# Gate and up projections of four feed-forward blocks by Strassen's seven products, down projection in three chunks

## The chip, the core and the metric

The kernel runs on one core of a Trainium2 chip. The metric is the device time of one execution in microseconds, the median of several. The core's engines run side by side, each in the order of its own list: TensorE (PE, with its weight loads, PEld), VectorE (DVE), ScalarE (ACT), GpSimd (POOL) and SyncE (SP), which issues the transfers. Tiles live in SBUF; TensorE writes into PSUM banks of 128 x 512 numbers.

## What is computed

A two-layer encoder on 512 tokens of width 1024. Each layer is feed-forward (ffn1), attention mixer, attention over a memory, feed-forward (ffn2). The change touches the four feed-forwards only:

```python
def swiglu(x, wg, wu, wd):
    return (jax.nn.silu(x @ wg) * (x @ wu)) @ wd
...
        h = h + 0.5 * swiglu(rmsnorm(h, g), wg, wu, wd)     # ffn1 and ffn2 of each layer, D_FF = 2816
```

## The kernel before

Activations lie transposed: eight tiles `x` of 128 features x 512 tokens. All products are float32 taken apart into two parts that TensorE multiplies fast: `xh` is the rounded tile (ACT), `xl` the rest (DVE), and weights likewise `wh` and `wl`. A product is three matmuls, wh·xh, wh·xl, wl·xh.

A weight tile of 128 x 1024 comes in `wload`: SP issues the transfer into `wf` (three buffers), ACT writes `wh` (L150), DVE writes `wl = wf - wh` (L152); `wh` and `wl` have two buffers each, so that a tile's parts can be made only when the matmuls of the tile two before it are done.

`ffn` runs over 22 blocks f of 128 hidden features. For each, 24 matmuls of 512 columns (8 feature tiles x 3) make the gate and 24 the up projection (L304), each from one weight tile into one bank. The first block's order follows the arrival of the `x` tiles. After the first 24 matmuls of block 1, `stats` transposes on TensorE (L244) the sums of squares `acc`, which ACT and DVE (or POOL) have added up over the eight `x` tiles; DVE reduces them (L246), POOL takes the root, TensorE spreads it over the partitions (L314), and DVE holds it as `R`. `gated` then makes the hidden block: gs = gate·R, tanh, w, us = up·R, h, and the parts `hh`, `hl`. Then `ffn` makes eight output blocks d of 66 matmuls each (L328), with the down weights in pieces of 8, 8 and 6 tiles of 128 x 128, adds the result to `x[d]` (L330), and `made` splits the new `x[d]` and adds its squares for the next norm.

TensorE's order is that of the code. The other engines' lists are set by a scheduler, which puts weight loading and splitting ahead (`high_priority`). Every engine works its list strictly in order. At the start `load_x` interleaves the eight `x` transfers with the first four half tiles of weights. Lines named L... are those of this kernel.

## Time and profile before

| | us |
|---|---|
| median of 3 runs | 2192.61 (2191.3 to 2194.66) |
| the profiled execution | 2188.73 |
| its span, first to last instruction | 2186.9 |

The profile is one execution. Busy times of TensorE are modelled: a matmul's row ends when its result is out, while the next one starts earlier, so the pace is read from starts. "The chain that ended last" follows the span back from its end to whatever released each step.

### The profile page before, as it was taken

What the parts mean: (1) busy time and instruction counts of PE and PEld (TensorE: products, weight loads), DVE (VectorE), ACT (ScalarE), POOL (GpSimd) and SP (SyncE); (2) the same over time, 40 slices, a digit from 0 to 9 for tenths busy, and PEclk for the clock granted to TensorE, in tenths of its full rate; (3) what the DMA queues carried; (4) which work ended last, traced back from release to release, by engine and by line L of the source; (5) the groups of instructions that cost most, each with busy time, mean ns of one, the idle gap of its engine ahead of it and who ended that gap; (6) DMA issues with size and microseconds to landing.
All of it is one profiled execution on the core that took longest, in us unless ns stands there. A gap on an engine that the chain in (4) does not pass through costs nothing.

```text
span 2186.9 us, 25743 instructions
## 1 busy us (share of the span) xinstructions
PE 2149.5 (98%) x9950; PEld 1785.1 (82%) x9954; DVE 1200.5 (55%) x1934; ACT 894.2 (41%) x1429; POOL 280.7 (13%) x227
## 2 busy tenths in 40 slices
PE   8999999999998999999999999999999989999999
PEld 7888888878787888888888888888888878888887
DVE  6555433479876665553335555334668677555422
ACT  5333223466675533332223332224678554333211
POOL 1000011345431100000000000013443010000000
PEclk9999999999999999999999999999999999999999
DMA  5222334222232132332332233334223212232232
GB/s 177 96 97 97 97 116 153 88 73 77 90 119 77 39 107 98 98 100 92 97 103 95 99 97 94 102 121 146 78 87 126 95 60 87 97 97 97 90 120 78
DMA packets 68811, 216.29 MB, mean 99 GB/s; under 512 B 7760, under 2 KB 10960, under 8 KB 68688
## 3 DMA queue, kind: packets, MB, share of 16 engines
q1 hardware_dynamic: 68688, 214.64, 30.3%
q8 instruction: 78, 1.28, 0.2%
q14 instruction: 45, 0.37, 0.1%
HBM read 208.32 MB, written 6.29 MB: 98 GB/s over the span
## 4 chain that ended last, share of the span: by engine, by line
PE 92%; DVE 6%; ACT 1%; issue 1%; DMA 0%; SPq 0%; DVEq 0%; ACTq 0%
PE ps_pa L304 23%; PE ps_pb L304 21%; PE ps_pb L328 11%; PE ps_pa L328 11%; PE ps_pa L403 10%; PE ps_pa L355 4%; PE ps_pb L509 2%; PE ps_pa L800 2%; PE ps_pa L941 2%; PE ps_pb L561 1%; PE ps_pa L719 1%; PE ps_pb L355 1%; PE ps_pb L534 1%; DVE sc L703 1%; DVE m L702 1%
## 5 line engine op out<-in xcount | busy, mean ns | idle before, releaser
L152 DVE TENSOR_TENSOR wl<-wf,wh 128x1024 fp32r<-128x1024 f32 (+2 forms) x333 | 398.0, 1197 | 611.6 <-ACT wh L150 309.5
L150 ACT ACTIVATE wh<-wf 128x1024 fp32r<-128x1024 f32 (+2 forms) x375 | 388.7, 1037 | 593.4 <-PE ps_pa L328 138.7
L304 PE MATMUL ps_pa<-xh,wh 128*128 128x512 f32 x736 | 186.0, 391 | 7.8 <-ACT wh L150 7.8
L304 PE MATMUL ps_pa<-xl,wh 128*128 128x512 f32 x736 | 185.9, 391 | 0.3 <-DVE xl L200 0.3
L304 PE MATMUL ps_pa<-xh,wl 128*128 128x512 f32 x736 | 181.3, 389 | 0.0
L304 PEld LDWEIGHTS ps_pa<-xh,wh 128*128 128x128 f32 x736 | 138.4, 189 | 36.8 <-ACT wh L150 7.8
L304 PE MATMUL ps_pb<-xh,wh 128*128 128x512 f32 x672 | 166.6, 390 | 0.0
L304 PE MATMUL ps_pb<-xh,wl 128*128 128x512 f32 x672 | 166.0, 389 | 0.0
L304 PE MATMUL ps_pb<-xl,wh 128*128 128x512 f32 x672 | 165.9, 389 | 0.0
L280 ACT ACTIVATE hh<-h 128x512 fp32r<-128x512 f32 x88 | 55.5, 631 | 267.2 <-DVE h L278 267.2
L304 PEld LDWEIGHTS ps_pa<-xl,wh 128*128 128x128 f32 x736 | 138.7, 188 | 30.2 <-DVE xl L200 1.4
L304 PEld LDWEIGHTS ps_pa<-xh,wl 128*128 128x128 f32 x736 | 138.2, 188 | 28.7
L217 POOL TENSOR_TENSOR acc<-acc,sq 128x512 f32<-128x512 f32 (+1 forms) x25 | 38.3, 1531 | 951.7 <-ACT sq L216 951.3
L272 ACT ACTIVATE t<-gs 128x512 f32<-128x512 f32 x88 | 55.6, 632 | 226.3 <-DVE gs L270 226.3
L304 PEld LDWEIGHTS ps_pb<-xl,wh 128*128 128x128 f32 x672 | 126.2, 188 | 26.2
L304 PEld LDWEIGHTS ps_pb<-xh,wl 128*128 128x128 f32 x672 | 126.1, 188 | 26.2
L304 PEld LDWEIGHTS ps_pb<-xh,wh 128*128 128x128 f32 x672 | 125.8, 188 | 26.0
L328 PE MATMUL ps_pb<-hh,wh 128*128 128x512 f32 x352 | 136.9, 389 | 0.0
L328 PE MATMUL ps_pb<-hh,wl 128*128 128x512 f32 x352 | 136.9, 389 | 0.0
L328 PE MATMUL ps_pa<-hh,wh 128*128 128x512 f32 x352 | 136.9, 389 | 0.0
L328 PE MATMUL ps_pa<-hh,wl 128*128 128x512 f32 x352 | 136.9, 389 | 0.0
L328 PE MATMUL ps_pa<-hl,wh 128*128 128x512 f32 x352 | 136.9, 389 | 0.0
(262 smaller groups left out, 3792.8 us busy)
## 6 DMA issues: line engine op xcount, KB each, us to landing
wf<-l_ffn_wg SPq DMA_DIRECT2D x87, 512.0 KB, 3.5
wf<-l_ffn_wu SPq DMA_DIRECT2D x87, 512.0 KB, 3.4
wf<-l_ffn_wd SPq DMA_DIRECT2D x64, 512.0 KB, 3.5
wf<-l_w_in SPq DMA_DIRECT2D x48, 512.0 KB, 3.5
wf<-l_ffn_wd SPq DMA_DIRECT2D x32, 384.0 KB, 3.0
wf<-l_mem_wkv SPq DMA_DIRECT2D x16, 512.0 KB, 3.5
wf<-l_w_out SPq DMA_DIRECT2D x16, 512.0 KB, 3.5
bias<-bias SPq DMA_DIRECT2D x28, 256.0 KB, 2.7
```

Of the source, the lines that this page charges most:

```text
L150: nc.scalar.activation(wh[:, sl], w[:, sl], AF.Copy)
L152: eng.tensor_sub(wl[:, sl], w[:, sl], wh.bitcast(F32)[:, sl])
L217: (eng or nc.gpsimd).tensor_add(acc[:, :n], acc[:, :n], sq[:, :n])
L272: nc.scalar.activation(t, gs, AF.Tanh, scale=0.5)
L280: nc.scalar.activation(hh, h, AF.Copy)
L304: nc.tensor.matmul(p, w[a][:, k * P:(k + 1) * P], xs[k][b], start=k == order[0] and a == b == 0, stop=k == order[-1] and a == 1)
L328: nc.tensor.matmul(p, a[:, j * P:(j + 1) * P], H[c + j][b], start=n == 0, stop=n == 3 * FB - 1)
L355: nc.tensor.matmul(banks[dd], a[:, o:o + P], parts(k)[b], start=k == first and a is wh and b == 0, stop=k == last and a is wl)
L403: nc.tensor.matmul(banks[i], xs[k][a][:, i * P:(i + 1) * P], w[b][:, kk * 512:kk * 512 + 512], start=k == a == b == 0, stop=k == KB - 1 an ...
L509: nc.tensor.matmul(bank[:, o:o + n], a, b[:, :n], start=c == 0, stop=c == len(ops) - 1)
L800: nc.tensor.matmul(banks[c][i], a[:, i * P:(i + 1) * P], b[:, c * 512:(c + 1) * 512], start=(k == 0 and n == 0), stop=(k == KB - 1 and n = ...
L941: nc.tensor.matmul(p, ws[z][a][:, k * P:(k + 1) * P], xs[k][b], start=k == order[0] and a == b == 0, stop=k == order[-1] and a == 1)
```

## The change

Hidden blocks 0 and 1 are made as before (`plain_pair`), the other twenty as ten pairs. A pair is a product of 2 x 2 quarters: outputs are (gate and up of block 0 or 1) x (tokens 0 to 255 or 256 to 511), the inner dimension is split in features 0 to 511 and 512 to 1023. Strassen's scheme (in Winograd's form) makes it with seven products of quarters instead of eight. A quarter of weights is one tile of 128 x 1024: 4 feature tiles x (gate, up) x 128. A product is 24 matmuls of 256 columns (gate and up x 3 parts x 4 feature tiles), gate and up into the two halves of one bank.

Sums of weights: `s` is loaded by SP, then a second transfer, issued by POOL, adds another quarter to it in place; DVE makes two further sums in the same tile. Sums of tokens (T1 to T4) are made once in each feed-forward, by `token_sums`. The down projection is done in three chunks of 8, 8 and 6 hidden blocks, the first two between the pairs, each with its own addition to `x`; the norm's factor R for the up half moves to there (`dn`).

```diff
+    def ffn(self, pre):
+            self.plain_pair()
...
+            pair = self.open_pair(1)
+            for p in range(1, FB // 2):
+                final = p == FB // 2 - 1
+                self.sum_pair(pair)
+                if p - 1 in [e - 1 for e in ends]:
+                    self.down(c)
+                    c += 1
+                self.cross_pair(pair, final)
+                old, pair = pair, None if final else self.open_pair(p + 1)
+                self.close_pair(old, final)
+            self.down(c)
...
+            if b == 0:
+                with self.behind(self.lead), self.behind(self.rest):
+                    self.token_sums()
...
+        def combine(out, k, tokens, op, other):
+            nc.vector.scalar_tensor_tensor(part(out, k), self.x[k][:, tokens], g(k), part(other, k), op0=OP.mult, op1=op)
...
+        for k in lead:
+            nc.scalar.activation(part(x12, k), self.x[k][:, two], AF.Copy, scale=g(k))
+        for k in lead:
+            combine(t1, k, one, OP.subtract, x12)
+        T1 = parts("t1", t1, -1.0)
...
+    def operand(self, t):
...
+        own = f.n % 3 == 2
+        f.n += 1
+        h, l = [(f.tp if own else self.wp).tile([P, 1024], F32R, name=n, tag=n, bufs=1 if own else 2)
+                for n in (("sh", "sl") if own else ("wh", "wl"))]
+        nc.scalar.activation(h, t, AF.Copy)
+        nc.vector.tensor_sub(l, t, h.bitcast(F32))
...
+    def product(self, bank, w, xs, first):
...
+        for z in range(2):
+            sl = slice(z * 256, z * 256 + 256)
+            for a, b in ((0, 0), (0, 1), (1, 0)):
+                for k in range(KB // 2):
+                    o = z * 512 + k * P
+                    self.nc.tensor.matmul(bank[:, sl], w[a][:, o:o + P], xs[k][b],
+                                          start=first and z == a == b == k == 0, stop=z == a == 1 and k == KB // 2 - 1,
+                                          skip_group_check=True)
...
+    def open_pair(self, p):
...
+            pair.w11 = self.raw_quarter(p, 0)
+            w = self.operand(pair.w11)
+        self.product(pair.y, w, f.B["11"], True)
...
+        nc.scalar.copy(self.corner(pair, 0, 0), self.halves(pair.y))
...
+    def sum_pair(self, pair):
...
+            pair.s = f.tp.tile([P, 1024], F32, name="s1", tag="s1", bufs=2)
+            nc.sync.dma_start(pair.s, self.quarter(p, 3))
+            nc.gpsimd.dma_start(pair.s, self.quarter(p, 2), accum_op=OP.add)
+            w = self.operand(pair.s)
+        self.product(pair.z, w, f.B["1"], True)
+        with self.tc.high_priority():
+            nc.vector.tensor_sub(pair.s, pair.s, pair.w11)
+            w = self.operand(pair.s)
+        self.product(pair.y, w, f.B["2"], False)
+        nc.scalar.copy(self.corner(pair, 0, 1), self.halves(pair.y))
...
+    def cross_pair(self, pair, final):
...
+                pair.w12 = self.raw_quarter(p, 1)
+                w = self.operand(pair.w12)
+            x = self.bank("pa")
+            self.product(x, w, f.B["21"], True)
+            c = self.corner(pair, 0, 0)
+            nc.vector.tensor_add(c, c, self.halves(x))
...
+                s = f.tp.tile([P, 1024], F32, name="s3", tag="s3", bufs=2)
+                nc.sync.dma_start(s, self.quarter(p, 2))
+                nc.scalar.activation(s, s, AF.Copy, scale=-1.0)
+                nc.gpsimd.dma_start(s, self.quarter(p, 0), accum_op=OP.add)
+                w = self.operand(s)
+            self.product(pair.y, w, f.B["3"], False)
+            c = self.corner(pair, 1, 1)
+            nc.scalar.copy(c, self.halves(pair.y))
+            nc.vector.tensor_add(c, c, self.halves(pair.z))
...
+    def close_pair(self, pair, final):
...
+                w = self.operand(self.raw_quarter(p, 3))
+            self.product(pair.y, w, f.B["4"], False)
+            nc.scalar.copy(self.corner(pair, 1, 0), self.halves(pair.y))
...
+                nc.vector.tensor_sub(pair.s, pair.w12, pair.s)
+                w = self.operand(pair.s)
+            self.product(pair.z, w, f.B["22"], False)
+            c = self.corner(pair, 0, 1)
+            nc.vector.tensor_add(c, c, self.halves(pair.z))
...
+    def down(self, c):
...
+                for a, e in ((0, 0), (1, 0), (0, 1)):
+                    nc.tensor.matmul(bank, w[a][:, j * P:(j + 1) * P], hs[e], start=j == a == e == 0, stop=j == nb - 1 and e == 1)
...
+            nc.vector.tensor_mul(t, bank, f.R)
+            nc.vector.scalar_tensor_tensor(self.x[d], t, 0.25, self.x[d], op0=OP.mult, op1=OP.add)
...
+        early = [block(d) for d in range(2)]
+        for w, bank in early:
+            products(bank, w, range(nb - 2))
+        for d, (w, bank) in enumerate(early):
+            products(bank, w, range(nb - 2, nb))
+            done(d, bank)
+        for d in range(2, KB):
+            w, bank = block(d)
+            products(bank, w, range(nb))
+            done(d, bank)
```

What this does to the lists is seen at three places. Lines of the changed kernel differ: L309 is L304 of before, L155 is L152, L203 is L200, L220 is L217, L193 is L190, L535 is a down matmul, L357, L364 and L366 are token sums and their rests.

SP at the start of the program, before (`x` are the eight input tiles, `wf` the first weights):

```order
L190 DMA x<-xT 128x512
L122 DMA cols<-cols 128x92
L190 DMA x<-xT 128x512
L149 DMA wf<-l_ffn_wg 128x512
L190 DMA x<-xT 128x512 x2
L149 DMA wf<-l_ffn_wu 128x512
L190 DMA x<-xT 128x512
L149 DMA wf<-l_ffn_wg 128x1024
L190 DMA x<-xT 128x512 x2
L149 DMA wf<-l_ffn_wg 128x512
L149 DMA wf<-l_ffn_wu 128x512
L190 DMA x<-xT 128x512
```

and after (`s_545`, `s_777`, `s_452`, `s_684` are tiles of weight sums of the first two pairs; the other four `x` and two halves of `wf` follow):

```order
L193 DMA x<-xT 128x512
L471 DMA s_545<-l_ffn_wq 128x1024
L193 DMA x<-xT 128x512
L471 DMA s_777<-l_ffn_wq 128x1024
L152 DMA wf<-l_ffn_wg 128x512
L193 DMA x<-xT 128x512
L125 DMA cols<-cols 128x92
L193 DMA x<-xT 128x512
L446 DMA s_452<-l_ffn_wq 128x1024
L152 DMA wf<-l_ffn_wu 128x512
L446 DMA s_684<-l_ffn_wq 128x1024
L152 DMA wf<-l_ffn_wg 128x1024
```

Four transfers of weight sums, 512 KB each, now stand ahead of the last four `x` tiles.

DVE at the start of ffn2 of layer 0, from the last four `xl` to the reduction `s` of TensorE's transposes of `acc`, before:

```order
L200 SCALAR_TENSOR_TENSOR xl<-x,cols,xh 128x512 x4
L152 TENSOR_TENSOR wl<-wf,wh 128x1024 x2
L217 TENSOR_TENSOR acc<-acc,sq 128x512 x3
L152 TENSOR_TENSOR wl<-wf,wh 128x1024
L217 TENSOR_TENSOR acc<-acc,sq 128x512
L152 TENSOR_TENSOR wl<-wf,wh 128x1024
L217 TENSOR_TENSOR acc<-acc,sq 128x512 x3
L152 TENSOR_TENSOR wl<-wf,wh 128x1024
L246 TENSOR_REDUCE s<-ps_pb 128x4
```

and after, the last twelve of 20 rows (ahead of them stand the four `xl`, three `wl`, two `acc` and eleven `tq`, the token sums):

```order
L155 TENSOR_TENSOR wl<-wf,wh 128x1024
L357 SCALAR_TENSOR_TENSOR tq<-x,cols,tq 128x256
L220 TENSOR_TENSOR acc<-acc,sq 128x512
L366 SCALAR_TENSOR_TENSOR t1l<-tq,t1h 128x1024
L357 SCALAR_TENSOR_TENSOR tq<-x,cols,tq 128x256
L364 TENSOR_TENSOR t3l<-tq,t3h 128x1024
L357 SCALAR_TENSOR_TENSOR tq<-x,cols,tq 128x256 x3
L399 TENSOR_TENSOR wl<-wf,wh 128x1024
L220 TENSOR_TENSOR acc<-acc,sq 128x512
L364 TENSOR_TENSOR t2l<-tq,t2h 128x1024
L364 TENSOR_TENSOR t4l<-tq,t4h 128x1024
L220 TENSOR_TENSOR acc<-acc,sq 128x512 x3
```

The additions to `acc` that came first now come after the token sums; TensorE's transposes of `acc` stand where they stood.

TensorE in the first down chunk, where output block 1 (bank `ps_pa_1222`) ends and block 2 begins, after (with buffer numbers; block 0 used `wh_1210`, and `wh_1278` is the next use of that buffer):

```order
L535 MATMUL ps_pb_1215<-hh_1143,wl_1211 128x512
L535 MATMUL ps_pb_1215<-hl_1144,wh_1210 128x512
L535 MATMUL ps_pa_1222<-hh_1143,wh_1217 128x512
L535 MATMUL ps_pa_1222<-hh_1143,wl_1218 128x512
L535 MATMUL ps_pa_1222<-hl_1144,wh_1217 128x512
L535 MATMUL ps_pa_1222<-hh_1143,wh_1217 128x512
L535 MATMUL ps_pa_1222<-hh_1143,wl_1218 128x512
L535 MATMUL ps_pa_1222<-hl_1144,wh_1217 128x512
L535 MATMUL ps_pb_1283<-hh_358,wh_1278 128x512
L535 MATMUL ps_pb_1283<-hh_358,wl_1279 128x512
```

Six matmuls lie between the last use of block 0's parts and the first of block 2's; before, a whole piece of 18 or 24 matmuls lay between.

## Rows read from the trace of the kernel before

**Rows 1.** The page: engines' busy time (share, instructions); the chain that ended last.

```profile
PE 2149.5 (98%) x9950; PEld 1785.1 (82%) x9954; DVE 1200.5 (55%) x1934; ACT 894.2 (41%) x1429; POOL 280.7 (13%) x227
...
PE 92%; DVE 6%; ACT 1%; issue 1%; DMA 0%; SPq 0%; DVEq 0%; ACTq 0%
```

**Rows 2.** Windows: length, engines' busy us (instructions), granted clock, DMA share, GB/s.

```profile
core 0: us, PE busy (x) PEld busy (x) DVE busy (x) ACT busy (x) POOL busy (x), PEclk, DMA share, GB/s
...
1121.70:1481.80 360.10, 360.10 (x1594) 298.26 (x1593) 165.84 (x198) 106.89 (x128) 11.82 (x7) 1.00 0.32 102
```

**Rows 3.** The chain in order of time: start, length, what it consists of.

```profile
92.63 5.44 PE ps_pa L304 x24
...
1106.85 14.96 PE ps_pb L328 x66
```

**Rows 4.** Timeline, memory attention: start, us, instruction; twelve 256-column matmuls end here.

```profile
713.97 0.28 PE L885 MATMUL ps_pb<-mkh,xql 128*128 128x256 f32 x1
713.97 0.19 PEld L885 LDWEIGHTS ps_pb<-mkl,xqh 128*128 128x128 f32 x1
...
715.15 0.28 PE L885 MATMUL ps_pb<-mkl,xqh 128*128 128x256 f32 x1
```

**Rows 5.** DVE's groups by form: xcount, busy us, mean ns, idle before.

```profile
L152 DVE TENSOR_TENSOR wl<-wf,wh 128x1024 fp32r<-128x1024 f32 x297 | 364.6, 1229 | 502.3 <-ACT wh L150 200.3 <-PE ps_pa L304 153.2 <-PE ps_pb L304 148.1
...
L796 DVE SCALAR_TENSOR_TENSOR ml<-mem,cols,mh 128x256 fp32r<-128x256 f32 x16 | 7.7, 489 | 5.5 <-ACT mh L794 5.4
```

**Rows 6.** ACT's groups by form, the weight split.

```profile
L150 ACT ACTIVATE wh<-wf 128x1024 fp32r<-128x1024 f32 x339 | 359.1, 1060 | 483.9 <-PE ps_pa L328 121.2 <-PE ps_pb L328 113.6 <-PE ps_pa L304 77.6
```

**Rows 7.** Timeline of DVE, start of ffn2 of layer 0.

```profile
764.13 2.73 DVE L200 SCALAR_TENSOR_TENSOR xl<-x,cols,xh 128x512 fp32r<-128x512 f32 x4
...
784.16 1.23 DVE L152 TENSOR_TENSOR wl<-wf,wh 128x1024 fp32r<-128x1024 f32 x1 [3.90 <-PE ps_pa L304]
785.30 0.68 DVE L316 COPY R<-ps_pb 128x512 f32<-128x512 f32 x1
786.02 0.69 DVE L270 TENSOR_TENSOR gs<-ps_pa,R 128x512 f32<-128x512 f32 x1
786.63 0.68 DVE L276 TENSOR_TENSOR us<-ps_pa,R 128x512 f32<-128x512 f32 x1
```

**Rows 8.** Timeline of TensorE at the same place.

```profile
777.98 0.60 PE L244 MATMUL ps_pb<-ident,acc 128*128 128x128 f32 x4
```

**Rows 9.** Timeline, end of ffn2 of layer 0 and start of ffn1 of layer 1.

```profile
1106.89 1.06 ACT L150 ACTIVATE wh<-wf 128x1024 fp32r<-128x1024 f32 x1 [3.02 <-PE ps_pa L328]
1106.89 0.69 DVE L330 SCALAR_TENSOR_TENSOR x<-ps_pa,x 128x512 f32<-128x512 f32 x1 [1.76 <-PE ps_pa L328]
...
1107.98 1.23 DVE L152 TENSOR_TENSOR wl<-wf,wh 128x1024 fp32r<-128x1024 f32 x1 [0.40 <-ACT wh L150]
...
1124.09 0.75 DVE L200 SCALAR_TENSOR_TENSOR xl<-x,cols,xh 128x512 fp32r<-128x512 f32 x1
...
1137.98 0.60 PE L244 MATMUL ps_pb<-ident,acc 128*128 128x128 f32 x4
```

**Rows 10.** Timeline, start of the program: the last `xl`, the transposes of `acc`.

```profile
14.92 0.75 DVE L200 SCALAR_TENSOR_TENSOR xl<-x,cols,xh 128x512 fp32r<-128x512 f32 x1
...
25.98 0.60 PE L244 MATMUL ps_pb<-ident,acc 128*128 128x128 f32 x4
```

**Rows 11.** Windows at the start of the program, columns as in Rows 2.

```profile
8.00:10.00 2.00, 2.00 (x5) 1.34 (x6) 1.96 (x4) 1.92 (x4) 0.00 (x0) 1.00 1.04 416
```

**Rows 12.** Timeline of TensorE in memory attention of layer 1, around a wait.

```profile
1769.02 0.96 PE L244 MATMUL ps_pb<-ident,acc 128*128 128x128 f32 x4 [4.63 <-DVE acc L217]
1769.63 3.47 PE L941 MATMUL ps_pa<-xh,wh 128*128 128x512 f32 x8
1772.94 1.98 PE L941 MATMUL ps_pa<-xl,wh 128*128 128x512 f32 x8
```

**Rows 13.** Windows right after that wait, columns as in Rows 2.

```profile
1769.00:1772.60 3.60, 3.58 (x11) 3.01 (x12) 1.03 (x3) 0.59 (x1) 1.01 (x1) 0.53 0.06 22
```

**Rows 14.** The page: transfers issued, count, size, us to landing.

```profile
wf<-l_ffn_wg SPq DMA_DIRECT2D x87, 512.0 KB, 3.5
```

238 lines of the change are left out of this document (168 added, 70 removed).

## Prediction

> **What bounds the kernel now.** I read the page first: TensorE is busy 98% of the span and holds 92% of the chain that ended last; VectorE is at 55%, ScalarE at 41% [rows 1]. An average hides stages, so next comes the window over a whole feed-forward: TensorE busy 360.10 of 360.10 us, granted clock 1.00 (the 2.4 GHz level), transfers at 0.32 of their engines' time [rows 2]. Inside it the chain in order of time is TensorE alone: 24 matmuls of 512 columns take 5.44 us, 66 take 14.96, both 226.7 ns a step [rows 3]. The feed-forwards end when the stream of matmuls ends, so fewer columns are worth their full time, unless an operand or a transposition comes late.
>
> **The change, part by part.** Six terms move the time; sums are made against the profiled execution, 2188.73 us.
>
> *The stream.* Two hidden blocks cost 96 x 226.7 ns = 21.76 us now. A pair costs 7 x 24 = 168 matmuls of 256 columns, each with weights of its own. Such matmuls stand in the memory attention: from 713.97 to 715.15 there are ten steps, 118 ns each, the weight loads beneath them starting at the same distance and lasting 0.19 each [rows 4]. So 168 x 118 = 19.82 us, 1.94 less. Over ten pairs and four feed-forwards: **-77.5 us**. Half of the long step is 113 ns and gives -108; 121 ns gives -57. The gain is a small rest of two large numbers: 6720 short matmuls, 6.7 us for each nanosecond, nothing left at 129.5. I take 118, the only measured step of this shape. The down matmuls stay 528 in number and 512 columns wide.
>
> *Start of ffn2, twice.* TensorE needs `acc` after the first 72 matmuls. Before, the last `xl` run ends at 766.86 [rows 7] and the transposes come at 777.98 [rows 8], without a wait. In the new order DVE first works, between the last `xl` and the last `acc`, five `wl` and four rests of token sums, sixteen token sums and seven additions. A `wl` lasts 1229 ns [rows 5], but starts overlap: next instruction after 1.14 (784.16 to 785.30); a 512-wide sum has a period of 0.60 (786.02 to 786.63) [rows 7]. Sixteen sums of 256 columns at 0.40 (0.489 for the like [rows 5], less that overlap of 0.09) are 6.4. So 9 x 1.14 + 7 x 0.60 + 6.4 = 20.9, ready at 787.8, 9.8 late; each turn of `wh` (1060 ns [rows 6]) fits beneath. Two such starts: **+20** (13 to 26). Block 1's other matmuls stand behind those transposes on TensorE, so nothing fills the wait.
>
> *Start of the program.* The last `xl` begins at 14.92 and the transposes at 25.98 [rows 10]. Four transfers of 512 KB now go ahead of the last `x`; at the 416 GB/s of that stretch [rows 11] they are 2.1 MB, 5.2 us. The additions by transfer may compete too; nothing shows that, between 0 and another 5.2, and I take 1.3. The last `xl` is then over at about 22.2. DVE has behind it seven `wl` and rests (8.0), seven `acc` (4.2), sixteen sums (6.4), small ones (0.7): 41.5 instead of 26.0, **+15.5** (10 to 22).
>
> *Start of ffn1 in layer 1.* Here the order leaves the `acc` additions ahead of the token sums. From the last `xl`, 1124.09 + 0.75 [rows 9], DVE has 15.0 to the reduction at 1139.8, whose transposes come at 1137.98 and whose result TensorE wants some 6 us later: **0**.
>
> *The clock after these waits.* Before, a wait of 4.63 us in front of the same transposes is followed by eight matmuls in 3.47 us where the next eight take 1.98 [rows 12], and the window over the 3.60 us shows a granted clock of 0.53 [rows 13], the 1.2 GHz level. That is 1.5, with the transposes 1.7. Three waits: **+5** (0 to 8).
>
> *Down in chunks.* A pair of weight buffers comes free when the matmuls of its tile are done. With two output blocks interleaved at a chunk's start, six matmuls, 1.36 us, lie between the last use of block 0's parts and the first of block 2's. ScalarE's `wh` takes 1.06 and DVE, having `dn` and the addition to `x` (0.69 each) ahead, ends `wl` 1.23 [rows 9] later, about 2.6 after block 0; `wl` is needed at 1.59. One microsecond in the eight chunks of eight tiles and 0.75 in the four of six: **+11** (0 to 16). A fall of the clock may follow too; a wait of 1 us has no row, so I leave it at nothing. At the ends of feed-forwards the last pair has no other pair's product between its steps: about 0.4 each and one `dn`, **+2**.
>
> *The steady pair.* Per pair of 19.8 us DVE has thirteen 1024-wide (1.14) and three 512-wide (0.60) instructions, 16.6 us, or 18.0 by full durations; ScalarE ten and four, 13 to 15. Both fit. Seven transfers of 512 KB instead of four make 185 GB/s; the start reached 416. A plain one lands in 3.5 us [rows 14]. One that adds into what lies there has no row: it can hardly be quicker than 3.5, and I bound it at three times that, 10.5. The tile is made some pairs' steps ahead (two tiles each of s1 and s3), so both are hidden. For what slips: **+2** (0 to 20).
>
> Sum: -77.5 + 20 + 15.5 + 5 + 11 + 2 + 2 = -22. On 2188.73 that is 2166.7 for a profiled execution; the median lies 3.9 above its profile, so 2192.6 - 22 = **2171 us**, -1.0%.
>
> **The rivals.**
>
> *Slower: the operand chain.* Two of the seven weight sums are made in place on DVE, from the tile that the previous operand has just been split from. Sum 1.23, `wh` 1.06, `wl` 1.23 are 3.5 us in a row, and a product lasts 2.83. If such a chain starts only when the product before it starts, 0.69 is missing twice a pair, 1.4 x 40 = 55 us: 2226. For it: DVE is to be 84 to 91% full, and its list is in strict order, so that one late instruction holds all. Against: three buffers of operands give a lead of two products, 5.7 us. From 0.55 us a pair (22 / 40) the kernel is slower than before.
>
> *Faster: the starts don't wait.* If the schedule's token sums turn out to be through in time, or the transfers at the start don't delay `x`, then 15.5 + 20 + 5 fall away: 2130. Against it stands that every list is worked in order, and in the list the additions stand last.
>
> *Slower: weight loads set the pace.* A load lasts 0.19 [rows 4]. In the memory attention loads overlap each other, with starts 118 apart; if in long runs they could not, a pair would take 168 x 0.19 = 31.9 us, 10.1 more than now, +404 and with the other terms about 2650. Slower than before from 121.3 ns a step on (118 + 22 / 6.72). The measured ten steps speak against it, but it is ten steps, not 6720. The Trainium skill, "TensorE: Matmul & The Clock Gate", section "LDWEIGHTS (loading the stationary operand)", gives columns / 1.2 in ns, so 107 for 128 columns, and its Part 3 says that a load overlaps running matmuls only where the row group differs. By that a short matmul would cost 107 + 107 = 214 ns and the pairs about +567 us. Rows 4, with 118 ns between starts under full-height weights, disagree.
>
> **How the numbers follow.** About 0.2% (4.4 us) is what a measurement of this kernel can tell from no change. The forecast gets 0.75: its own terms, each at its ends with the others held and the deviations combined by squares, span 2150 to 2198; of the 0.75, 0.64 is faster, 0.07 within 0.2%, 0.04 slower. The operand chain gets 0.14, the pace of loads 0.04, the starts without a wait 0.07 (faster). Together: faster 0.71, same 0.07, slower 0.22. The range holds the forecast, the second rival at its low end, and on top the lighter part of the first, late in three quarters of the pairs or less: 2130 to 2212.
>
> **What the changed kernel's profile would show.** Right: a product of 24 short matmuls in 2.8 to 2.9 us in the chain; TensorE waiting some 10 us for `acc` ahead of the transposes in both ffn2, later by 15 at the program's start, not in layer 1's ffn1; a granted clock near one half for a few us behind each; a wait near 1 us at the third block of a down chunk; DVE at 84 to 91% in the pairs' windows. Wrong, if a product takes 3.1 us or more with TensorE unbroken (the step), if TensorE waits inside pairs for `wl` or for a summed `s` (the chain, or the adding transfers), or if the transposes find `acc` ready.

## The result, and the profile of the changed kernel

The change made the kernel slower: 2213.68 us (median of 4 runs, 2211.45 to 2214.58) against 2192.26 us, a ratio of 1.0098 with an interval of 1.0086 to 1.011. The profiled spans are 2212.6 and 2186.9 us, 25.7 apart; the medians are 21.4 apart. The forecast was 2171 us, and its range ended at 2212. (Executions of one kernel differ: those of the kernel before on record took 2187.91 to 2194.66 us, and the profiled one, 2188.73, is among the fastest. So some 4 us of the 25.7 need not be the change's.)

The page of the changed kernel, answering to [rows 1]: busy time of each engine with its share and its number of instructions, then the chain that ended last by engine.

```profile
PE 2111.8 (95%) x12830; PEld 1881.5 (85%) x12834; DVE 1573.5 (71%) x2255; ACT 1139.7 (52%) x1701; POOL 339.6 (15%) x306
...
PE 88%; DVE 7%; DMA 2%; ACT 1%; issue 1%; SPq 0%; DVEq 0%; ACTq 0%
```

TensorE works 38 us less than before and the kernel takes 26 us more. So some 63 us of idle TensorE were added, and the rest of the reading is a search for them. The mean granted clock, 0.997 before and 0.984 now, tells that idleness is not all of it: part of the busy time is work at a lower clock.

**The stream of short matmuls is as long as one row says it is.** The chain in order of time (start, length, what it consists of), answering to [rows 3]:

```profile
68.10 14.40 PE ps_pa L417 x120
...
88.26 14.40 PE ps_pa L417 x120
```

120 matmuls of 256 columns in 14.40 us are 120.0 ns a step; 168 of them in a pair make 20.16 us, and that is the distance between the two rows. The head of a product, the first one in ffn1 of layer 0, in TensorE's timeline (start, length, instruction, number in the group, idle time before it and its releaser):

```profile
62.12 0.71 PE L417 MATMUL ps_pa<-xh,wh 128*128 128x256 f32 x4 [1.41 <-DVE R L320]
62.66 0.64 PE L417 MATMUL ps_pa<-xl,wh 128*128 128x256 f32 x4
```

The first group takes 0.54 us, since its first step is 194 ns long; the others follow at 0.48, four steps of 120. The first product waits 1.41 us for the copy of R out of its bank; inside steady pairs nothing waits. The window over the pairs of the second feed-forward (length, then PE, PEld, DVE, ACT, POOL busy with instructions, granted clock, share of the transfers, GB/s), answering to [rows 2]:

```profile
818.00:888.00 70.00, 70.00 (x572) 69.32 (x571) 57.58 (x56) 40.35 (x47) 5.21 (x6) 1.00 0.60 160
```

TensorE is busy 70.00 of 70.00 us, VectorE at 82%. The transfers that add are hidden too; the page gives for the plain ones and for the adding ones (queue, count, size, us from issue to landing), answering to [rows 14]:

```profile
s<-l_ffn_wq SPq DMA_DIRECT2D x80, 512.0 KB, 4.2
s<-l_ffn_wq POOLq DMA_DIRECT2D x80, 512.0 KB, 6.8
```

**The loss stands at the seams.** TensorE's waits (what it waited for; us in total, times, longest):

```profile
PE ps_pb L247 <- DVE acc L220: 38.8, 5, 10.3
PE ps_pa L309 <- ACT xh L201: 15.4, 3, 11.4
PE ps_pa L309 <- ACT wh L153: 8.2, 3, 5.6
PE ps_pa L535 <- DVE wl L155: 5.4, 6, 1.0
PE ps_pb L535 <- DVE wl L155: 5.4, 6, 1.0
PE ps_pa L417 <- ACT gu L454: 4.8, 4, 1.2
PE ps_pa L417 <- DVE R L320: 3.0, 2, 1.6
```

Of the first group two waits, 9.5 us together, belong to the memory attention and were there before; the three new ones are 9.19 at the start of the program, 10.34 and 9.74 in the two ffn2. Of the second group the 11.4 is the start of the program, until the first matmul; before, that wait was 7.83. The rest of the list is new.

The timeline at the start of ffn2 of layer 0, answering to [rows 8]:

```profile
782.86 1.06 ACT L472 ACTIVATE s<-s 128x1024 f32<-128x1024 f32 x1
784.77 0.70 ACT L201 ACTIVATE xh<-x,cols 128x512 fp32r<-128x512 f32 x1
785.53 0.50 PE L309 MATMUL ps_pa<-xh,wh 128*128 128x512 f32 x1 [2.04 <-ACT xh L201]
...
812.86 1.11 PE L247 MATMUL ps_pb<-ident,acc 128*128 128x128 f32 x4 [10.34 <-DVE acc L220]
813.63 3.76 PE L309 MATMUL ps_pa<-xh,wh 128*128 128x512 f32 x8
```

Two waits are to be seen. The long one is the forecast one: the transposes of `acc` come when DVE is through with the token sums. The short one was not forecast: ScalarE's change of sign (L472) for the second pair's weight sum stands in its list ahead of an `xh` that TensorE needs at once. Another one, for the first pair, stands ahead of it at 779.70 and had waited 0.53 us for its transfer. Behind the long wait eight matmuls take 3.76 us where eight like them take 1.98. The windows of the same stretch (columns as above):

```profile
803.00:806.00 3.00, 0.00 (x0) 0.00 (x0) 3.00 (x6) 0.41 (x1) 0.00 (x0) 1.00 0.33 127
...
808.00:810.00 2.00, 0.00 (x0) 0.00 (x0) 2.00 (x2) 0.63 (x1) 0.00 (x0) 0.50 0.00 0
...
817.00:818.00 1.00, 1.00 (x3) 0.75 (x3) 0.00 (x0) 0.00 (x0) 0.00 (x0) 0.50 0.00 0
818.00:819.00 1.00, 1.00 (x6) 0.79 (x5) 0.00 (x0) 0.00 (x0) 0.00 (x0) 0.99 0.00 0
```

TensorE's last matmul ahead of the wait ends at 802.5. The granted clock goes to 0.50 (the 1.2 GHz level) at about 808, while TensorE still waits, and comes back at 818: ten microseconds, of which the last five fall on work and cost half their length.

At the start of the program, answering to [rows 10], the list of waits puts 11.40 us ahead of the first matmul (7.83 before), then 2.36 and 5.63 for weights and 9.19 for `acc`; the transposes come at 51.34 where they came at 25.98. The last `xl` on VectorE and the transposes:

```profile
30.59 0.75 DVE L203 SCALAR_TENSOR_TENSOR xl<-x,cols,xh 128x512 fp32r<-128x512 f32 x1
51.34 1.09 PE L247 MATMUL ps_pb<-ident,acc 128*128 128x128 f32 x4 [9.19 <-DVE acc L220]
```

The last `xl` ends at 31.34, where it ended at 15.67.

In the down projection, at the third output block of a chunk, and at the end of the last pair of a feed-forward (timeline of TensorE):

```profile
901.72 0.50 PE L535 MATMUL ps_pa<-hh,wh 128*128 128x512 f32 x1
903.16 0.51 PE L535 MATMUL ps_pa<-hh,wl 128*128 128x512 f32 x1 [0.94 <-DVE wl L155]
```

```profile
343.41 0.75 PE L417 MATMUL ps_pa<-t3h,wh 128*128 128x256 f32 x4 [1.20 <-ACT gu L454]
```

From start to start the wait for `wl` is 1.44 us. A step without a wait is 0.23 and the idle row shows 0.94; the other 0.27 the row does not show, since the matmul before it is counted as busy for 0.50 us, until its result is out, while the next would have started after 0.23. This wait costs that much more than its row.

### The profile page after: what moved, and what is told of

Its sections match the earlier page's. It is cut to its first block, busy times and chain, and to the rows that moved or that the text cites. A ratio compares the mean times of both kernels' runs of the same rounds, so it can differ in the third digit from the quotient of the medians.

```text
span 2212.6 us, 32535 instructions
## 1 busy us (share of the span) xinstructions
PE 2111.8 (95%) x12830; PEld 1881.5 (85%) x12834; DVE 1573.5 (71%) x2255; ACT 1139.7 (52%) x1701; POOL 339.6 (15%) x306
## 4 chain that ended last, share of the span: by engine, by line
PE 88%; DVE 7%; DMA 2%; ACT 1%; issue 1%; SPq 0%; DVEq 0%; ACTq 0%
PE ps_pa L417 26%; PE ps_pb L535 11%; PE ps_pa L535 10%; PE ps_pb L417 10%; PE ps_pa L628 10%; PE ps_pa L580 4%; PE ps_pa L309 2%; PE ps_pb L734 2%; PE ps_pa L1166 2%; PE ps_pa L1025 2%; PE ps_pb L786 1%; PE ps_pb L759 1%; PE ps_pa L944 1%; PE ps_pb L309 1%; PE ps_pb L580 1%
## 5 line engine op out<-in xcount | busy, mean ns | idle before, releaser
L153 ACT ACTIVATE wh<-wf 128x1024 fp32r<-128x1024 f32 (+2 forms) x215 | 219.1, 1019 | 380.5 <-PE ps_pb L535 112.7
L155 DVE TENSOR_TENSOR wl<-wf,wh 128x1024 fp32r<-128x1024 f32 (+2 forms) x174 | 202.9, 1168 | 63.6 <-ACT wh L153 62.9
L399 DVE TENSOR_TENSOR wl<-s,wh 128x1024 fp32r<-128x1024 f32 x104 | 127.2, 1223 | 86.5 <-ACT wh L398 64.1
L398 ACT ACTIVATE wh<-s 128x1024 fp32r<-128x1024 f32 x104 | 110.0, 1058 | 114.5 <-PE ps_pb L417 29.4
L535 PE MATMUL ps_pb<-hh,wl 128*128 128x512 f32 x352 | 137.8, 392 | 5.4 <-DVE wl L155 5.4
L535 PE MATMUL ps_pa<-hh,wl 128*128 128x512 f32 x352 | 137.8, 392 | 5.4 <-DVE wl L155 5.4
L535 PE MATMUL ps_pb<-hh,wh 128*128 128x512 f32 x352 | 137.6, 391 | 0.0
L535 PE MATMUL ps_pa<-hh,wh 128*128 128x512 f32 x352 | 137.5, 391 | 0.0
L535 PE MATMUL ps_pa<-hl,wh 128*128 128x512 f32 x352 | 137.3, 390 | 0.0
L535 PE MATMUL ps_pb<-hl,wh 128*128 128x512 f32 x352 | 137.3, 390 | 0.0
L155 POOL TENSOR_TENSOR wl<-wf,wh 128x1024 fp32r<-128x1024 f32 x41 | 99.7, 2431 | 176.4 <-ACT wh L153 148.9
L628 PE MATMUL ps_pa<-wh,xh 128*128 128x512 f32 x384 | 123.3, 402 | 0.0
L628 PE MATMUL ps_pa<-wh,xl 128*128 128x512 f32 x384 | 119.9, 394 | 0.0
L628 PE MATMUL ps_pa<-wl,xh 128*128 128x512 f32 x384 | 119.5, 393 | 0.0
L399 DVE TENSOR_TENSOR wl<-wf,wh 128x1024 fp32r<-128x1024 f32 x84 | 102.6, 1222 | 0.0
```

The costliest lines, as they stand in the source:

```text
L153: nc.scalar.activation(wh[:, sl], w[:, sl], AF.Copy)
L155: eng.tensor_sub(wl[:, sl], w[:, sl], wh.bitcast(F32)[:, sl])
L398: nc.scalar.activation(h, t, AF.Copy)
L399: nc.vector.tensor_sub(l, t, h.bitcast(F32))
L535: nc.tensor.matmul(bank, w[a][:, j * P:(j + 1) * P], hs[e], start=j == a == e == 0, stop=j == nb - 1 and e == 1)
L628: nc.tensor.matmul(banks[i], xs[k][a][:, i * P:(i + 1) * P], w[b][:, kk * 512:kk * 512 + 512], start=k == a == b == 0, stop=k == KB - 1 an ...
```

## The experiments

Unless another is named, the kernel changed is the one of the diff. The differences in us are between its 2213.68 us and the experiment's median; the ratios are to the kernel before on the same chip.

### Four seams, each undone alone

**Token sums behind the additions to `acc`.**

```diff
-                with self.behind(self.lead), self.behind(self.rest):
+                with self.behind(self.sq_last), self.behind(self.add_last):
                     self.token_sums()
```

> The token sums on VectorE and ScalarE are queued behind the last addition to acc, in all four feed-forwards; nothing else changes. Theory: in three starts TensorE waits for acc (9.19, 10.34 and 9.74 us in the trace of after) because the token sums stand ahead of it, and the lower clock behind each wait costs another 2.7 us; both go, 37 us, so 2177 us and no wait over 1 us ahead of the transposes of acc. Rival: the sums are only late elsewhere, at the second to fifth product of the first pair, which then wait for t1 to t4; then 15 us or less are gained (2198 or more) and the waits stand at the products.

Measured: 2194.84 us, ratio 1.0018 (1.0008 to 1.0028), 18.8 us less; about half of what was hoped for. The waits view shows why:

```profile
PE ps_pa L318 <- POOL r L240: 6.6, 1, 6.6
PE ps_pb L318 <- POOL r L240: 5.4, 2, 2.7
```

The three new waits for `acc` are gone, and three others stand a few steps on. TensorE spreads the root `r` over the partitions, POOL makes the root from `v`, and `v` stands in DVE's list behind the token sums, which now come right after the last addition. The wait moved by one link of the chain.

**The last `x` tiles ahead of the first weight sums.**

```diff
+            with self.behind(self.last_x if self.first_ffn else None):
                 nc.sync.dma_start(pair.s, self.quarter(p, 3))
```

and the same at the second transfer of this kind (L471).

> At the start of the program the four transfers of weight sums are queued behind the last transfer of x. Theory: those transfers and ScalarE's sign changes, which wait for two of them, made the last xl end at 31.3 instead of 15.7 us; with them behind, TensorE's first matmul comes at 7.9 again and the transposes of acc 15 us earlier: 2199 us. Rival: x comes late because of other loads, or the wait for acc takes the gain back: 2208 or more.

Measured: 2199.92 us, ratio 1.0041 (1.0026 to 1.0056), 13.8 less. TensorE's timeline at the start of the program:

```profile
6.71 1.22 PE L312 MATMUL ps_pa<-xh,wh 128*128 128x512 f32 x2 [6.71 <-ACT wh L154]
...
37.83 1.09 PE L249 MATMUL ps_pb<-ident,acc 128*128 128x128 f32 x4 [9.93 <-DVE lam L1010]
```

The first matmul comes 4.7 us earlier and the transposes 13.5; the wait ahead of the transposes itself stays. The last `xl` ends at 16.15, against 31.34. So four transfers of 512 KB ahead of `x`, with the sign changes that wait for two of them, cost more than the transfers' own 5.2 us at the stretch's rate.

**The change of sign behind the last `xh`.**

```diff
-                nc.scalar.activation(s, s, AF.Copy, scale=-1.0)
+                with self.behind(f.lead if p < 3 else None):
+                    nc.scalar.activation(s, s, AF.Copy, scale=-1.0)
```

> ScalarE's sign change of the third weight sum of the first two pairs is queued behind the last xh in every feed-forward. Theory: at the starts of both ffn2 ScalarE's list held a sign change that waited for its transfer ahead of an xh, and TensorE waited 2.04 and 2.01 us for it; at the start of the program two of them stood ahead of all xh. These go: 4 us in both ffn2 and up to 4 at the program's start, 2206 us. Rival: the wait for acc behind it is set by VectorE, which isn't held by this, so it grows by as much: 2213 us.

Measured: 2201.86 us, ratio 1.005 (1.0035 to 1.0065), 11.8 less. The two waits for `xh` in ffn2 are gone from the list; only the program's start is left in it:

```profile
PE ps_pa L309 <- ACT xh L201: 10.7, 1, 10.7
```

The 4.1 us of these two waits do not make 11.8. At the program's start the first matmul comes 0.7 us earlier, and the phase from there to the pairs became 4.4 us shorter (46.34 instead of 50.72), since the sign change stood in the way there too. The same phase of ffn2 is 3.3 us shorter in layer 0 (35.89 for 39.23), but only 0.9 in layer 1 (36.97 for 37.91), where the rival came true in part: the wait for `acc` grew from 9.74 to 12.31 us.

```profile
1860.69 1.12 PE L247 MATMUL ps_pb<-ident,acc 128*128 128x128 f32 x4 [12.31 <-DVE acc L220]
```

Half the time that TensorE worked at 0.50 is 14.5 us in the profiled execution, 21.9 in that of the changed kernel; part of it lies within these phases, the rest was not measured apart.

**The first two output blocks of a chunk with more matmuls between them.**

```diff
-        for w, bank in early:
-            products(bank, w, range(nb - 2))
-        for d, (w, bank) in enumerate(early):
-            products(bank, w, range(nb - 2, nb))
+        part = (nb - 2, nb - 4)
+        for (w, bank), n in zip(early, part):
+            products(bank, w, range(n))
+        for d, ((w, bank), n) in enumerate(zip(early, part)):
+            products(bank, w, range(n, nb))
```

> In each chunk of the down projection the second output block of the interleaved start does four hidden blocks less ahead of the first one's end, so that 12 matmuls instead of six (2.7 us for 1.36) lie between the last use of the first block's weights and the third block. Theory: the waits of 0.74 to 1.0 us for wl at the third block in all 12 chunks go, 11 us: 2203 us. Rival: the hidden blocks made last (hh, hl) aren't ready when the first block wants them, since 1.4 us less work lies ahead; the waits move there and nothing is gained.

Measured: 2202.25 us, ratio 1.0054 (1.0039 to 1.0069), 11.4 less. In the chunks of eight tiles the start-to-start excess at the third block goes from 1.37 to 0.05 us; that the fault was the distance of six matmuls is shown. In the chunk of six only two tiles of block 1 are then left ahead, and a wait stands there for the last hidden blocks, 4.1 us in the four of them, so that the rival holds there:

```profile
PE ps_pb L535 <- ACT hh L344: 2.2, 2, 1.2
```

### The clock, and the pace of the matmuls

**Work in the waits for `acc`.** 40, 44 and 42 matmuls whose result is thrown away stand ahead of the transposes, as long as the waits, so that TensorE does not stand still.

```diff
+        for _ in range(busy):
+            nc.tensor.matmul(p, h[:, :P], h, start=True, stop=True)
```

> The changed kernel with 40, 44 and 42 matmuls of 512 columns more, whose results are thrown away, ahead of the transposes of acc in the three starts that wait; they last 9.1, 10.0 and 9.5 us, as long as the waits of 9.2, 10.3 and 9.7. Theory: the waits cost their length and, through the lower clock behind them, about 2.7 us each more (the 28 steps behind the transposes take 7.6 to 7.8 us for 5.5); with TensorE busy meanwhile the clock stays and some 8 us go: 2205 us. Rival: the slow steps behind a wait are slow for another reason (operands late): 2214, or more where the extra matmuls run past the wait.

Measured: 2206.03 us, ratio 1.0069 (1.0055 to 1.0083), 7.7 less, as the theory of the clock said. TensorE's timeline in ffn2 of layer 0 and the window there:

```profile
800.24 10.14 PE L249 MATMUL ps_pb<-xh 128*128 128x512 f32 x44
...
810.57 2.06 PE L313 MATMUL ps_pa<-xh,wh 128*128 128x512 f32 x8
```

```profile
808.00:818.00 10.00, 10.00 (x56) 8.49 (x55) 4.05 (x7) 1.70 (x2) 1.04 (x1) 1.00 0.00 1
```

The transposes come no earlier, but the eight matmuls behind them take 2.06 us instead of 3.76, and the granted clock is 1.00 where it was 0.50. So the clock behind these three waits is a loss of its own beside the waits: from the first matmul to the pairs the three starts became 2.5, 1.9 and 1.5 us shorter, some 6 of the 7.7. Where the rest lies isn't shown; the attention stages have less time at 0.50 in this execution too.

**Half the columns.**

```diff
-                    self.nc.tensor.matmul(bank[:, sl], w[a][:, o:o + P], xs[k][b],
+                    n = 256 if k == a == b == 0 else 128
+                    self.nc.tensor.matmul(bank[:, z * 256:z * 256 + n], w[a][:, o:o + P], xs[k][b][:, :n],
```

> In each product 18 to 22 of 24 matmuls use 128 of the 256 columns, the weights are loaded as before; half of the product's work is left out, so the time is not the kernel's. It tells what makes the step of 120 ns. Theory: one column per cycle of the 2.4 GHz level and a fixed part, as 226.7 ns for 512 and 120.0 for 256 columns give (106.7 per 256 columns and 13.3 for each matmul): 66.7 ns for 128. Rival: a fresh load of weights can't follow the last one sooner than about 118 ns, whatever the columns: then the step stays at 118 to 120 and the products keep their 2.88 us.

Measured once: 2351.23 us, so with nearly half of the products' columns left out (22 of each 24 matmuls have 128) it is 138 us slower in that one execution. The chain (start, length, content) has two levels of it, and the window (columns as above) tells which is which:

```profile
70.36 25.60 PE ps_pa L418 x120
...
245.45 13.46 PE ps_pa L418 x120
```

```profile
100.00:140.00 40.00, 40.00 (x190) 40.00 (x189) 20.50 (x19) 13.46 (x16) 1.73 (x2) 0.50 0.35 94
```

The first thing to see is that at the upper clock 120 steps, ten of them still with 256 columns, take 13.46 us, 112.2 ns each. Neither theory's number came: by columns alone 128 would take 66.7, and a pace of weight loads at 120 would have left 120. There is a floor of about 112 ns under the steps, and a step of 256 columns at 120.0 lies only 8 ns above it. That the loads make the floor is likely, since each step brings new weights, but no run kept the weights standing, so it isn't shown. The 256-column step is not set by the floor: from it to the 512-column one (226.7) 256 columns more take 106.7 ns, which is a column in 0.417 ns or 2.4 GHz, and each has 13.3 ns besides (106.7 + 13.3, 213.3 + 13.3).

The second is the time at 0.50: from 62.9 to 185.8 us the granted clock stayed at the lower level while TensorE had these matmuls without a gap, 213.3 ns each. It rose some 3 us after the down projection's matmuls of 512 columns had begun at 183.00. A second stretch as long stands in ffn1 of layer 1, from 1240.5 to 1363.4. In another stretch (205 to 390) the same products ran at 1.00. What tells the two stretches apart was not settled.

### Towards a version that is faster

**Token sums behind `v`**, the answer to the first experiment's new wait.

```diff
+                        with self.behind(self.sq_last), self.behind(self.v_last):
+                            self.token_sums()
```

> As the run with the late token sums, but these are queued behind v, the step of VectorE that follows the reduction of the transposed acc, rather than behind the last addition to acc. Theory: in that run 6.58, 2.73 and 2.72 us of the wait only moved, from the transposes of acc to those of r, because token sums stood ahead of v in VectorE's list; with v ahead of them R is in time and the first products' t1 to t4 still are: 2177 us. Rival: VectorE has too little time for token sums between v and the second product; the wait moves on to the products of the first pair and the time stays near 2195.

Measured: 2208.17 us, ratio 1.0076 (1.0061 to 1.0092), only 5.5 less. The theory fell: the sums put off as a whole come too late for what follows them.

```profile
PE ps_pb L247 <- POOL acc L220: 6.6, 1, 6.6
PE ps_pa L416 <- ACT sh L397: 8.0, 2, 4.0
PE ps_pa L416 <- DVE sl L398: 5.1, 2, 2.6
```

The operand of the third product (`sh`, `sl`) waits behind them, and so do the statistics of the memory; ffn1 of layer 1, where nothing but a short wait for R had been lost, gets a wait of 3.9 us.

**All mends together**: sums behind `v`, `x` first, sign late, the down chunk (with one tile less put off in the last chunk), and another bank for R.

```diff
+                        with self.behind(self.sq_last), self.behind(self.v_last):
+                            self.token_sums()
+        self.pflip ^= 1
+        p = self.bank("pb")
...
+                with self.behind(f.lead if p < 3 else None):
+                    nc.scalar.activation(s, s, AF.Copy, scale=-1.0)
...
+        part = (nb - 2, nb - (3 if last else 4))
```

> All of it together: token sums behind v, the first transfers of weight sums behind x, the first sign changes behind the last xh, four hidden blocks less (three in the last chunk) ahead in the second output block, and R's transposes always in a bank of the other set than the first product's. Theory: the gains add up where they concern different waits: 37 for the token sums, 14 for x first, 7 for the sign changes in both ffn2 (at the program's start they are contained in x first), 12 for the down chunks, 3 for the bank: 73 us off 2214, 2140 us. Rival: the starts share one chain on VectorE, so that the gains there overlap: 2155 or more.

Measured: 2191.86 us, ratio 1.0002 (0.9994 to 1.0011). 52 us too slow for the expectation: the parts do not add up, since what one of them gave back at a seam was waited for at the next.

```profile
PE ps_pa L420 <- ACT sh L401: 13.0, 3, 4.9
PE ps_pb L249 <- POOL acc L222: 9.2, 1, 9.2
```

**Less work for DVE at the start**: two of the token sums and their rests go to ScalarE and POOL, a part of the weights' rests to POOL, and the statistics of the memory come later.

```diff
-            combine(t3, k, two, OP.subtract, x12)
-        T3 = parts("t3", t3)
+            nc.scalar.activation(part(t3, k), self.x[k][:, two], AF.Copy, scale=g(k))
+        nc.gpsimd.tensor_sub(t3, t3, x12)
+        T3 = parts("t3", t3, eng=nc.gpsimd)
```

> The combined version, with VectorE relieved at the starts: of the token sums, T3 and T4 are scaled on ScalarE and added and split on GpSimd (four instructions of 1024 columns), GpSimd also makes wl of hidden block 1, and the statistics of the memory are taken after the first down chunk. Theory: in the combined version the starts were late because VectorE had more work between the last xl and the third product (t2, the in-place sum and its parts) than TensorE has matmuls; some 6 to 8 us of it are taken off, against waits of 9.0, 6.4 and 9.2 us in the last three starts, and the statistics' wait of 9.2 us in the first start goes. With the lower clock behind them 30 us off 2192: 2162 us, faster than before. Rival: the third product is late because of the chain of one operand after the other (sum, then ScalarE's part, then VectorE's), not for the amount of work; then the waits at t2 stay and 2180 or more is measured.

Measured: 2193.84 us, ratio 1.0009 (1.0 to 1.0018): nothing gained over the run before. The later statistics took their wait of 9.2 us away at the program's start (10 us less up to the pairs), but both ffn2 reach the pairs 2.5 and 4.7 us later. Since two things were changed at once, the run does not show whether the amount of DVE's work binds; the next one does. The waits have other names now:

```profile
PE ps_pb L423 <- DVE t1l L370: 8.4, 2, 4.4
PE ps_pa L423 <- ACT gu L443: 7.5, 3, 3.7
```

The second is a pointer. `gu`, the copy that frees a bank, has no data from the token sums; but its tile shares its buffers (the tag "gu") with the tiles in which the token sums are made, and has to wait until the rests of the token sum in its buffer are done.

**The sums in the order in which they are needed.** T1 and T2 right behind the last addition to `acc`; their rests and T3, T4 behind `v`; the rests of T3 and T4 behind the third product's weights; the tiles in the order `t1, t2 | x12, t3`, so that `gu` gets the one that is free early; ffn1 of layer 1 as in the changed kernel; otherwise the mends of the combined kernel, with the memory's statistics later.

```diff
-        x12, t1, t2, t3 = (t[:, o:o + 1024] for t in room for o in (0, 1024))
+        t1, t2, x12, t3 = (t[:, o:o + 1024] for t in room for o in (0, 1024))
...
+        with self.behind(first):
+            for k in lead:
+                combine(t1, k, one, OP.subtract, x12)
+            for k in rest:
+                combine(t2, k, two, OP.add, t1)
...
+        with self.behind(rest_after):
+            T1 = parts("t1", t1, -1.0)
+            T2 = parts("t2", t2)
...
+        def late():
+            f.B["3"] = parts("t3", t3)
+            f.B["4"] = parts("t4", t4)
```

> The combined version with VectorE's list put in the order of need, the same work on the same engines: in the three starts whose acc comes late the sums T1 and T2 stand behind the last addition to acc, their rests and the sums T3 and T4 behind v, the rests of T3 and T4 behind the parts of the third product's weights; the first pair's gu takes the tile of T1 and T2, not that of T4. Layer 1's ffn1 keeps its order, and the memory's statistics come after the first down chunk. Theory: order and the shared gu tile, not the amount of work, made the combined version's starts late (waits of 9.2, 9.0, 6.4 and 9.3 us for acc, sh, sl); what is due before the third product in ffn2 is some 19 us on VectorE for 16.6 on TensorE behind the transposes, of which 3 fit ahead: 2192 less 34 us of waits and 15 us of lower clock, plus 4 for what is left, 2150 us, faster than before. Rival: VectorE is simply full in the starts (relieving it in another way gave nothing); then 2180 or more and the waits stand at the second and third products again.

Measured: **2169.33 us, ratio 0.9901 (0.9885 to 0.9918)**, faster than both kernels, though 19 us above the expectation. That it lies near the 2171 forecast for the changed kernel is chance: that was worked out for other lists. The page, and TensorE's timeline in ffn2 of layer 0:

```profile
PE 2104.4 (97%) x12830; PEld 1878.6 (87%) x12834; DVE 1574.0 (73%) x2255; ACT 1138.1 (53%) x1701; POOL 344.6 (16%) x306
```

```profile
779.26 0.66 PE L249 MATMUL ps_pb<-ident,acc 128*128 128x128 f32 x4 [2.58 <-DVE acc L222]
```

DVE does as much as in the changed kernel (1574.0 and 1573.5 us) and TensorE has the same 12830 instructions. Order (of transfers too), banks and buffers differ, and they are worth 44 us. So the amount of DVE's work alone is not what made the starts late. The wait for `acc` is 2.58 instead of 10.34; mean granted clock 0.992. What is left at the third product is 7.0 us for `sh` in three waits.

**The same with the old order of tiles.**

```diff
-        t1, t2, x12, t3 = (t[:, o:o + 1024] for t in room for o in (0, 1024))
+        x12, t1, t2, t3 = (t[:, o:o + 1024] for t in room for o in (0, 1024))
```

> The ordered version with one thing undone: the first pair's gu takes again the tile in which T4 is summed, so that the copy of the first product out of its bank, and with it the third product (which adds into that bank), has to wait for the rests of T4. Theory that both order and tile counted: the third product of the first pair waits in the three starts for that copy, some 5 us more each with a lower clock behind: 2185 us or more. Rival: the order alone did it, the tile costs nothing: 2169 us.

Measured: 2180.61 us, ratio 0.9951 (0.9938 to 0.9963). One line that names tiles is worth 11 us. Another 11 lie between the combined kernel (2191.86) and this one, but they are not the order of the sums alone: the memory's statistics come later too, and the program's start is 9.2 us shorter up to the pairs (30.35 for 39.53), as long as the wait of 9.2 us that the statistics had there. What the order gives without the tiles was not measured apart. The wait that the old tile brings back:

```profile
PE ps_pa L432 <- ACT gu L452: 17.8, 3, 6.2
```

**Transfers of weight sums behind the plain weights, in ffn2.**

```diff
-            with self.behind(self.last_x if self.first_ffn else None):
+            with self.behind(f.late_w if p < 3 else None):
                 nc.sync.dma_start(pair.s, self.quarter(p, 3))
```

and the same at the second transfer of this kind; the sign changes stand behind the split of T1.

> The ordered version, and in both ffn2 the first four transfers of weight sums are queued behind the last transfer of the plain pair's weights, with the sign changes behind the split of T1 on ScalarE. Theory: in the ordered version ScalarE waits 5 us for the weights of hidden block 1 (up), which stand behind those transfers in SP's queue and hold up the squares, and that is why TensorE still waits 2.58 and 2.92 us for acc in both ffn2; both waits and the lower clock behind them go, 9 us: 2160 us. Rival: the weights come late because of their buffer, not the queue; then acc is as late as before, and the sums of the first pair may now be late too: 2169 or more.

Measured: 2168.33 us, ratio 0.9891 (0.9876 to 0.9906), not to be told from the 2169.33 of the ordered sums. The waits for `acc` in ffn2 are gone, and their time stands at the next links, the root (2.7 us in the ordered kernel) and the first pair's weights (2.7 us for a `wl`):

```profile
PE ps_pb L327 <- POOL r L242: 5.9, 2, 3.7
```

## Why the prediction was wrong

The mechanism was as forecast: fewer column-steps in the stream, paid for at the starts of feed-forwards. But the gain is a small rest of large numbers, and it was outweighed. In the order of the sum, each term in us of the two profiled executions:

| term | predicted | measured |
|---|---|---|
| stream, 40 pairs | -77.5 | -64.0 |
| start of the program | +15.5 | +20.8 |
| waits for `acc`, both ffn2 | +20 | +20.1 |
| waits for `xh`, both ffn2 | 0 | +4.1 |
| wait for the bank of R, both ffn1 | 0 | +3.0 |
| third block of the down chunks | +11 | +10.8 |
| last pairs | +2 | +4.8 |
| clock | +5 | +17 |
| steady pairs | +2 | 0 |
| refilling after a wait | 0 | +6.8 |
| sum | -22 | +23.4 |

2.3 us of the 25.7 are assigned to none. So the gain, put at 77.5, came to 64.0, and the costs, put at 55.5, came to 87.4. Four steps of the prediction failed: the length of a step, the arrival of `x` at the program's start, the waits and the refilling that were put at nothing, and the clock.

*The stream* was mis-sized by 13.5 us. The step is 120.0 ns, not 118. The ten steps of [rows 4] stood at the head of a run, and the step ahead of them was not read:

```profile
713.76 0.36 PE L885 MATMUL ps_pb<-mkh,xqh 128*128 128x256 f32 x1
```

From here to 713.97 it is 0.20 us, and the steps behind it are shorter than those of a long run; all eleven make 126 ns on average. In the changed kernel it is the same: behind the wait for R the first step takes 194, the next nine 116 to 122, 118 on average, and after that each takes 120.0. With 6720 steps the two nanoseconds are 13.4 us. The 120.0 lay inside the bounds that were taken, and by it alone the forecast would have been 2184.5, still faster.

*The starts.* Both ffn2 came out at 10.34 and 9.74 where 9.8 was worked out from DVE's list. At the program's start DVE's list was read rightly too: from the end of the last `xl` to the transposes it takes 20.0 us, where 19.3 were worked out. What failed is the arrival of `x`: the last `xl` was to be over at 22.2 and was over at 31.34, since the competition for the transfers was put too low. The transposes come 25.4 us later than before, for the 15.5 forecast. The idle rows of it are the 20.8 of the table: 3.6 us up to the first matmul, which nothing was set down for, and 2.36, 5.63 and 9.19 after it; the rest is in the rows for clock and refilling. The second experiment gave 13.8 back by the order of the transfers alone.

*The short waits not looked for* are the waits for `xh`, for R's bank and the larger part of the last pairs. Each was to be read from the order of the lists: a sign change ahead of an `xh`, R's copy from the bank that the first product takes, a copy `gu` ahead of t3's product. Only DVE's list had been followed at the starts, not ScalarE's, nor the banks.

*The clock* is the second largest miss, 12 us. Half the length of the stretches in which TensorE worked at 0.50 is 17 us more than before. The three long waits, to which the 5 were tied, make some 7; the experiment with work in the waits gave 7.7 back, some 6 of it at these places. The other 10 stand behind shorter waits, for which the term held nothing: 3.6 at the program's start, 1.4 in ffn2 of layer 1, and 4.9 in the attention stages, which the change does not touch. There the same wait of 1.54 us had a granted clock of 1.00 behind it before, and 0.57 now. The windows behind it (columns as above), first before, then after:

```profile
1792.50:1796.00 3.50, 3.50 (x18) 2.98 (x19) 1.90 (x6) 2.79 (x9) 0.31 (x1) 1.00 0.02 5
```

```profile
1811.00:1815.00 4.00, 4.00 (x13) 3.28 (x14) 2.27 (x7) 2.79 (x9) 0.32 (x1) 0.57 0.02 4
```

What decides whether a short wait is followed by a fall stays open. The kernel before has mean granted clocks of 0.994 to 0.997 on record, and 0.997 in the profiled execution, so the 4.9 us may be the difference of two executions and not the change's.

*Refilling* was no term at all: 25 new waits (three at the start, two and two in ffn2, two for R, twelve in the down chunks, four in last pairs) at the 0.27 us that the row at 903.16 leaves, an estimate from that one row.

*The rivals.* None came as told. The operand chain did not: steady pairs have no wait, as in the window of 70.00 of 70.00 us with DVE at 82%, just under the 84 to 91 that was worked out. (Where the token sums come later, the first pair's third product does wait for its operand, `sh` and `sl`, but only at the starts.) The pace of loads did not, though the experiment with half the columns shows a floor as near as 112 ns, where steps take 120.0. By the Trainium skill, "TensorE: Matmul & The Clock Gate", section "LDWEIGHTS (loading the stationary operand)", a load of 128 columns is some 107 ns. The floor of 112.2 lies 5 above it. Part 3 of the same page of the Trainium skill says that a load overlaps running matmuls only where the row group differs. The 120.0 over 6720 steps, with loads of 128 x 128 under each, does not agree with that. And the starts did wait.

*The range.* Its terms were combined by squares, as though they were independent. Of the eight terms that missed by more than 1 us seven lean the same way, and six of these are waits or what follows from waits: one that isn't looked for can only add. A term for what the lists hold and the reading missed would have had to be positive; the two waits predicted at 0 and the refilling alone make 14 us. The slower case had been given to one mechanism inside the pairs, while the price was at the seams, where the sum itself had placed all but 2 of its 55.5 us of costs.

## What to carry to other kernels

When a change pays at the seams of a stream, follow every engine's list and every bank and buffer there, also those of tiles that merely share a tag: each wait that is not looked for adds, none subtracts, and the clock behind it adds again. A wait that is taken away by moving work is found one link further on until the work stands in the order in which its results are needed; here order, banks and buffers were worth 44 us at the same work. A step that is to be multiplied by thousands is read from the middle of a long run, not from the first ten. And of two changes made in one run neither has a price of its own.

## What the runs showed of the hardware beyond what was expected

- Matmuls with new weights each time: 226.7 ns for 512 columns, 120.0 for 256, both the columns at 2.4 GHz plus 13.3; 112.2 a step where 110 of 120 have 128. Behind the wait for R the first step of 256 columns took 194 ns, the next nine 118 on average.
- In one execution TensorE, busy without a gap with matmuls mostly of 128 columns, was granted 0.50 for 122.9 us on end, twice, and less work took longer: 2351.23 us.
- After a wait of 10.34 us the granted clock was 0.50 for ten microseconds, which began some 5 us into the wait; with thrown-away matmuls in the wait it stayed at 1.00.
- A transfer of 512 KB that adds to what lies in SBUF lands in 6.8 us (median of 80), a plain one of the same tile in 4.2.
- The wait of 0.94 us at 903.16 cost 0.27 us more than its idle row tells.
